# Dilation-16 attention as 64x64 products per residue class and head

## The chip, the cores and the metric

The kernel runs on one core of a Trainium2 chip. The metric is the device time of one execution in microseconds; the median of the runs shown is compared. The core has TensorE (matrix products, in the profile PE, with its weight loads as PEld), VectorE (DVE), ScalarE (ACT), GpSimd (POOL) and SyncE (SP, which issues nearly all DMAs). They run at the same time and wait for one another on semaphores.

## What is computed

Two layers of a decoder trunk on 1024 positions of 1024 features: a dilated attention mixer, an MLP, a gated linear recurrence (HGRN2), an MLP, with a layer norm after each. The change is in the attention mixer alone. It has 16 heads of 64 features and three groups with (window, dilation) = (128, 1), (512, 4), (2048, 16); the group outputs are mixed by their softmax denominators.

```
def dilated_window_attention(q, k, v, window, dilation):
    blk = window // dilation
    ...
    qb, kb, vb = to_blocks(q), to_blocks(k), to_blocks(v)   # one sequence per residue class mod dilation
    kk, vv = with_prev(kb), with_prev(vb)
    s = einsum('znqhe,znkhe->znhqk', qb, kk) * (E ** -0.5)
    s = where(valid, s, -inf)              # 0 <= distance <= blk, key exists
    m = max(s); p = exp(s - m); l = sum(p)
    o = einsum('znhqk,znkhe->znqhe', p / l, vv)
    lse = m + log(l)
```

With dilation 16 the 1024 positions fall into 16 residue classes of 64 positions. The window covers a whole class, so each class is one causal 64x64 attention and no block has a predecessor.

## The kernel before

The attention mixer is 24 units: eight pairs of heads times three dilations, in the order 16, 4, 1 within a pair (`GORD`). Two consecutive units make a group. While TensorE computes the projections of one group (21 products of twelve 128x512 passes each, lines 750 to 752), the attention work of the group before is put between these products: `unit_work` gives a list of steps, and `OFFS` says behind which product each one goes, two products (24 passes) apart. TensorE and DVE execute in the order in which the code writes them (`in_order`); ACT and SP take their instructions as the scheduler laid them.

A unit holds queries and keys of two heads with features on partitions: head 0 on partitions 0 to 63, head 1 on 64 to 127. For dilations 4 and 16 the positions are sorted by residue class, so a block of 128 columns is two classes of dilation 16. `pieces` does one unit:

- `qk` (scores, PSUM bank tag "s", two banks, one per head): for each of eight blocks b and each head a product with 64 rows of contraction and a 128x128 result. For dilation 16 half of that result is between two different classes and is masked away with the third part of `mask`. DVE (line 572) adds the mask, scales, and takes the row extreme into the statistics `sS`; ACT (line 575) takes the exponential and its row sum.
- `ptr` transposes the probabilities in four 128x128 transposes a call through a bank tagged "pt" (two banks) and copies them to an SBUF tile `pts` (line 587).
- `pv` multiplies them with the values: per block and head one product with 128 rows of contraction, 64 result partitions and 128 columns (line 598), into the one bank "o"; behind every fourth block ACT copies the bank to `og` (line 609).
- `vtrans` transposes the values (lines 545 and 546).

For dilation 16 the six steps of a unit are: 0 scores of blocks 0 to 3 and `vtrans`; 1 scores of blocks 4 to 7 and the eight transposes of the first half; 2 nothing; 3 value products of the first half and transposes of the second; 4 nothing; 5 value products of the second half. Step 5 falls on the same place as step 0 of the next unit.

`combine_tr` then transposes the statistics (line 648), writes them to DRAM (`mdram`) and reads them back in natural order into `ml`, with four DMAs on SP for dilation 16 (line 658); `combine` and `combine_mul` mix the three groups of a pair later.

Two lines outside the attention are used below: in the recurrence (`omat`) the code writes per 128 positions two products at line 1718, one to the left and one to the right 64 columns of the array, then the same two at line 1723 with the running state; in the first 128 positions only the right one of these.

In the profile an f32 product shows as two passes, an f32 transpose as one. PE shapes read as rows\*columns of the array, then the moving operand.

Of the kernel before, what the change touches and what calls it, by code (L numbers as in the profile page):

```python
# [9 lines left out]
F32 = mybir.dt.float32  # L10
F32R = mybir.dt.float32r
U8 = mybir.dt.uint8
AF = mybir.ActivationFunctionType
ALU = mybir.AluOpType
AX = mybir.AxisListType

P = 128
# [3 lines left out]
HD = 64  # L21
# [48 lines left out]
def trunk_kernel(  # L70
# [24 lines left out]
    nc = tc.nc  # L95
    cp = ctx.enter_context(tc.tile_pool(name="cp", bufs=1))
    up = ctx.enter_context(tc.tile_pool(name="up", bufs=NSLOT))
    wp = ctx.enter_context(tc.tile_pool(name="wp", bufs=3))
# [7 lines left out]
    def bank(tag, name):  # L106
        return ps.tile([P, 512], F32, name=name, tag=tag, bufs={"mm": 3, "s": 2, "pt": 2, "o": 1}[tag])

    def small(shape, name, bufs=4, dt=F32):
        return sp.tile(shape, dt, name=name, tag=name, bufs=bufs)  # L110

    act = nc.scalar.activation
# [31 lines left out]
    ident = cp.tile([P, P], F32, name="ident")  # L144
# [212 lines left out]
    def attention(pre, hc):  # L357
# [136 lines left out]
                v = nc.vector  # L494
                v.tensor_sub(H[n][:, R], lows.pop(n), H[n][:, L].bitcast(F32))  # L495

        mask = cp.tile([P, 384], F32, name="mask")
        sel = cp.tile([P, NG * P], F32R, name="bsel")
        frow = U("frow", F32R)
        mdram = dp.tile([NPAIR, NG, 2, 2, S], F32, name="mdram")  # L500
# [32 lines left out]
        def pieces(pr, g, qT, kT, vT, og, sS, tail):  # L533
            st = {}

            def has_prev(b):
                return (g == 0 and b > 0) or (g == 1 and b % 2 == 1)
# [11 lines left out]
            def qk(*tiles):  # L549
                sb = [bank("s", "s") for _ in range(2)]  # L550
                at, c0 = {}, 0
                for b in sum(tiles, ()):
                    prev = has_prev(b)
                    n = 256 if prev else 128
                    k0 = (b - 1 if prev else b) * P
                    at[b] = slice(c0, c0 + n)
                    c0 += n
                    for h in range(2):
                        nc.tensor.matmul(sb[h][:, at[b]], qT[h * HD:(h + 1) * HD, b * P:(b + 1) * P],  # L559
                                         kT[h * HD:(h + 1) * HD, k0:k0 + n], start=True, stop=True,  # L560
                                         skip_group_check=True)
                for tile_ in tiles:
                    whole = wp.tile([P, 512], F32, name="p", tag="p")
                    st["p", tile_] = whole
                    for i, b in enumerate(tile_):
                        prev = has_prev(b)
                        n = 256 if prev else 128
                        m = mask[:, 0:256] if prev else (mask[:, 256:384] if g == 2 else mask[:, 128:256])
                        p = [whole[:, (2 * i + h) * n:(2 * i + h + 1) * n] for h in range(2)]
                        for h in range(2):  # L570
                            nm = sS[:, 0, h, b:b + 1]
                            nc.vector.tensor_tensor_reduce(p[h], sb[h][:, at[b]], m, -0.125, 3.0e38,  # L572
                                                           op0=ALU.add, op1=ALU.min, accum_out=nm)
                        for h in range(2):
                            act(p[h], p[h], AF.Exp, bias=sS[:, 0, h, b:b + 1], scale=-1.0,  # L575
                                accum_out=sS[:, 1, h, b:b + 1])

            def ptr(tile_):
                pt = bank("pt", "ppt")
# [32 lines left out]
            def qks(*tiles):  # L612
                return [lambda: qk(*tiles)]

            def run(f, bs):
                return [lambda b=b: f(b) for b in bs]
# [10 lines left out]
                ]  # L627
            first, second = run(pv, range(4)), run(pv, range(4, 8))
            if g == 2:
                two = [(b, b + 1) for b in range(0, 8, 2)]  # L630
                return [qks(*two[0:2]) + [vtrans], qks(*two[2:4]) + run(ptr, two[0:2]), [],
                        first + run(ptr, two[2:4]), [], second]
            if g == 1:
                return [qks((0, 2), (4, 6)) + [vtrans], qks((1,), (3,)) + run(ptr, ((0, 2), (4, 6))),
                        qks((5,), (7,)) + run(ptr, ((1,), (3,))), first + run(ptr, ((5,), (7,))), [], second]
# [4 lines left out]
        def combine_tr(pr, g, slot, ml, tail):  # L640
            pt = bank("pt" if tail else "o", "mpt")
            q0 = slot * 32
            if DIL[g] == 1:
                for w in range(2):
                    nc.tensor.transpose(pt[:, w * P:w * P + P], allS[:, 16 * w:16 * w + P], ident)
                act(ml[:, :, 0, :], pt[0:16, 0:2 * P].rearrange("p (w t) -> p w t", w=2), AF.Copy)
                return
            nc.tensor.transpose(pt[:, 0:P], allS[:, 0:P], ident)
            sr = small([P, P], "sr", 2)
            act(sr[q0:q0 + 32], pt[q0:q0 + 32, 0:P], AF.Copy)  # L650
            yield
            md = mdram[pr, g]
            d = DIL[g]
            nc.scalar.dma_start(md.rearrange("w h (b q) -> (w h b) q", q=P), sr[q0:q0 + 32])
            yield
            for w in range(2):
                for h in range(2):
                    nc.sync.dma_start(
                        ml[8 * h:8 * h + 8, w, g, :].rearrange("i (r n) -> i r n", r=d),
                        md[w, h].rearrange("(r i n) -> i r n", r=d, i=8))  # L660
            yield

        def combine(pr, ml):
# [67 lines left out]
        ml, ogs = {}, {}  # L731
# [116 lines left out]
        for n in range(len(seq)):  # L848
            gi, i, j = seq[n]
# [1005 lines left out]
    pr = Out(w_attn_out, "a", 0)  # L1855
    hc = []
    oN, fill = attention(pr.pre_steps, hc)
    gw = GateW()
    f = ffn(0, x1d, ln_ffn_g[0], ln_ffn_b[0], False, (gw.ask, lambda: gw.prefetch(0)))
# [6 lines left out]
    f = ffn(1, x5d, ln_ffn_g[1], ln_ffn_b[1], True)  # L1866
# [6 lines left out]
def _constants():  # L1873
    import numpy as np

    f = np.float32
    half = HD // 2
    inv = (f(10000.0) ** (-np.arange(half, dtype=f) * f(2.0 / HD))).astype(f)
    ang = inv[:, None] * np.arange(S, dtype=f)[None, :]
    c, s = np.cos(ang).astype(f), np.sin(ang).astype(f)  # L1880
    cos_t = np.concatenate([c, c, c, c], 0)
    sin_t = np.concatenate([-s, s, -s, s], 0)
    qi = np.arange(P)[:, None]
    kj = np.arange(P)[None, :]
    neg = f(-1.0e30)
    prev = np.where(kj >= qi, f(0), neg)
    own = np.where(kj <= qi, f(0), neg)
    pk = np.where((kj <= qi) & (kj // 64 == qi // 64), f(0), neg)
    masks = np.concatenate([prev, own, pk], 1).astype(f)
    cm = ((kj >= qi) & (kj // CH == qi // CH)).astype(f)  # L1890
    cmask = np.tile(cm, (1, 4))
    sm = np.ones((P, S), f)
    sm[:, ::CH] = 0.0
    rows = np.arange(P)[:, None]
    bsel = np.concatenate([((rows // 4 == g) & (rows % 2 == np.arange(P)[None, :] // HD)).astype(f)
                           for g in range(NG)], 1)
    return {"cos_t": cos_t, "sin_t": sin_t, "masks": masks, "cmask": cmask, "smask": sm, "bsel": bsel}
# [49 lines left out]
```

## Time and profile before

| | |
|---|---|
| median of 3 runs | 2762.18 us (2761.52 to 2764.75) |
| profiled execution, first to last instruction (its own time as far as the profile shows it) | 2759.7 us |
| TensorE busy | 2734.4 us, 99% |
| DVE, ACT busy | 2076.6 us (75%), 1419.4 us (51%) |
| chain that ended last | PE 92%, DVE 5% |
| attention stage with its projections | from the start to about 1000 us |
| score passes (line 559), all units | 768 passes, first 84.4, last 985.6 us |
| value passes (line 598), all units | 1120 passes, first 105.0, last 993.9 us |
| transposes of probabilities (line 584) | 560 |

A row of a timeline gives the start, the time from the start of the first to the end of the last instruction of the row, engine, line, operation and count. TensorE passes overlap, so the distance between starts is what a pass costs, and it is shorter than its own duration.

### The profile page before, as it was taken

Reading aid. Unit: us, or ns where it says so; the run is one execution under the profiler, and the core shown is the slowest. Engines: PE = TensorE matmul, PEld = TensorE weight load, DVE = VectorE, ACT = ScalarE, POOL = GpSimd, SP = SyncE. Lnnn points to the kernel's source line nnn. Section 1 sums busy time; section 2 is a strip of 40 time slices with the busy share of each in tenths; the row PEclk is TensorE's granted clock in tenths of the full one; section 3 lists DMA queues with packets and bytes.
Section 4 is the critical chain, followed back from the end, with each engine's and each line's share of the span. In section 5 each row is a group of like instructions: output and inputs, shape, how many; then the busy total and the mean of one; then the engine's idle time right before and its main releaser. Section 6 shows DMA issues by size and latency. Waiting matters only on the chain.

```text
span 2759.7 us, 40110 instructions
## 1 busy us (share of the span) xinstructions
PE 2734.4 (99%) x14312; PEld 2237.2 (81%) x14312; DVE 2076.6 (75%) x3876; ACT 1419.4 (51%) x3059; POOL 69.0 (2%) x46
## 2 busy tenths in 40 slices
PE   9999999999999999999999999999999999999998
PEld 7888888888888777888888888888888888888887
DVE  8868877777888768876696777565678887678687
ACT  5555555555555456445454435455552545455443
POOL 0000000000000001000000000010100100000000
PEclk9999999999999999999999999999999999999999
DMA  8767666766767324454584852001142464485654
GB/s 303 257 209 214 197 205 191 234 185 212 225 208 226 120 94 160 168 211 152 186 290 134 275 171 92 31 32 62 65 130 104 149 220 170 143 292 191 217 176 129
DMA packets 204041, 485.02 MB, mean 176 GB/s; under 512 B 28992, under 2 KB 42816, under 8 KB 203840
## 3 DMA queue, kind: packets, MB, share of 16 engines
q1 hardware_dynamic: 203072, 482.19, 52.6%
q8 instruction: 113, 1.85, 0.3%
q14 instruction: 88, 0.72, 0.1%
q10 hardware_dynamic: 768, 0.26, 0.0%
HBM read 362.69 MB, written 94.11 MB: 166 GB/s over the span
## 4 chain that ended last, share of the span: by engine, by line
PE 92%; DVE 5%; ACT 1%; issue 1%; DMA 1%; SPq 0%; POOL 0%; DVEq 0%; ACTq 0%; POOLq 0%
PE pmm L752 8%; PE pmm L750 8%; PE pmm L751 8%; PE pup L1272 7%; PE pup L1270 7%; PE pup L1271 7%; PE pdy L1421 4%; PE pdy L1425 4%; PE pdy L1424 4%; PE pdx L1424 3%; PE pdx L1425 3%; PE pdx L1421 3%; PE pmm L192 3%; PE pmm L194 3%; PE pmm L193 3%; PE s L559 3%
## 5 line engine op out<-in xcount | busy, mean ns | idle before, releaser
L750 PE MATMUL pmm<-xh,H 128*128 128x512 f32 x1008 | 402.1, 399 | 2.0 <-ACT H L487 1.9
L752 PE MATMUL pmm<-xh,H 128*128 128x512 f32 x1008 | 394.0, 391 | 2.3 <-DVE H L495 2.2
L751 PE MATMUL pmm<-xl,H 128*128 128x512 f32 x1008 | 393.0, 390 | 0.7 <-DVE xl L158 0.7
L752 PEld LDWEIGHTS pmm<-xh,H 128*128 128x128 f32 x1008 | 189.2, 188 | 44.9 <-DVE H L495 4.3
L750 PEld LDWEIGHTS pmm<-xh,H 128*128 128x128 f32 x1008 | 189.5, 188 | 40.4 <-ACT H L487 3.0
L751 PEld LDWEIGHTS pmm<-xl,H 128*128 128x128 f32 x1008 | 189.7, 188 | 37.7 <-DVE xl L158 1.1
L575 ACT ACTIVATE p<-p,stats 128x128 f32<-128x128 f32 (+1 forms) x384 | 167.9, 440 | 81.6 <-DVE stats L572 81.4
L1421 PE MATMUL pdy<-dT,dS 128*128 128x512 f32 x512 | 199.2, 389 | 0.0
L1424 PE MATMUL pdy<-dT,dS 128*128 128x512 f32 x512 | 199.2, 389 | 0.0
L1425 PE MATMUL pdy<-dT,dS 128*128 128x512 f32 x512 | 199.2, 389 | 0.0
L572 DVE CUSTOM_DVE_ANT_0 p<-s,mask 128x128 f32<-128x128 f32 (+1 forms) x384 | 111.1, 348 | 98.9 <-PE s L559 91.0
L157 ACT ACTIVATE dS<-dr 128x512 fp32r<-128x512 f32 x192 | 119.4, 622 | 69.9 <-PE pdy L1425 36.2
L192 PE MATMUL pmm<-f0nh,wh 128*128 128x512 f32 x384 | 153.2, 399 | 0.0
L194 PE MATMUL pmm<-f0nh,wl 128*128 128x512 f32 x384 | 149.8, 390 | 0.0
L193 PE MATMUL pmm<-f0nl,wh 128*128 128x512 f32 x384 | 149.7, 390 | 0.0
L158 DVE TENSOR_TENSOR dS<-dr,dS 128x512 fp32r<-128x512 f32 x192 | 131.5, 685 | 7.6 <-ACT dS L157 7.6
L157 ACT ACTIVATE dT<-hold 128x512 fp32r<-128x512 f32 x128 | 80.1, 626 | 78.5 <-DVE hold L1400 33.4
L1231 ACT ACTIVATE H<-wc 128x512 fp32r<-128x512 f32 x128 | 77.2, 626 | 77.6 <-DVE wc L1224 46.4
L1425 PEld LDWEIGHTS pdy<-dT,dS 128*128 128x128 f32 x512 | 96.1, 188 | 20.1
L1424 PEld LDWEIGHTS pdy<-dT,dS 128*128 128x128 f32 x512 | 96.1, 188 | 19.9
L1421 PEld LDWEIGHTS pdy<-dT,dS 128*128 128x128 f32 x512 | 96.1, 188 | 19.8
L587 ACT ACTIVATE pts<-ppt 128x512 f32<-128x512 f32 (+1 forms) x146 | 77.7, 575 | 44.4 <-PE ppt L584 44.1
(412 smaller groups left out, 6836.0 us busy)
## 6 DMA issues: line engine op xcount, KB each, us to landing
xh<-xtd SPq DMA_DIRECT2D x110, 512.0 KB
xl<-xtd SPq DMA_DIRECT2D x110, 512.0 KB
dr<-hd SPq DMA_DIRECT2D x192, 256.0 KB
dr<-in_w_down_dram SPq DMA_DIRECT2D x128, 256.0 KB
rot<-e SPq DMA_DIRECT2D x192, 128.0 KB
wa<-in_w_up_dram SPq DMA_DIRECT2D x48, 512.0 KB
wb<-in_w_attn_dram SPq DMA_DIRECT2D x36, 512.0 KB
wa<-in_w_attn_dram SPq DMA_DIRECT2D x33, 512.0 KB
```

Of the source, the lines that this page charges most:

```text
L157: act(hi, raw, AF.Copy)
L192: nc.tensor.matmul(o, wh[:, k], xs.h(k), start=k == 0, stop=False)
L193: nc.tensor.matmul(o, wh[:, k], xs.l(k), start=False, stop=False)
L194: nc.tensor.matmul(o, wl[:, k], xs.h(k), start=False, stop=k == NK - 1)
L750: nc.tensor.matmul(o, wh, hi[k // 2][:, c], start=begin and k == 0, stop=False, skip_group_check=True)
L751: nc.tensor.matmul(o, wh, lo[k // 2][:, c], start=False, stop=False, skip_group_check=True)
L752: nc.tensor.matmul(o, wl, hi[k // 2][:, c], start=False, stop=end and k == 3, skip_group_check=True)
L1270: nc.tensor.matmul(o, wh, xf.h(b, k), start=begin and k == 0, stop=False, skip_group_check=True)
L1271: nc.tensor.matmul(o, wh, xf.l(b, k), start=False, stop=False, skip_group_check=True)
L1421: nc.tensor.matmul(o[q], h, T_[:, L], start=begin, stop=False, skip_group_check=True)
L1424: nc.tensor.matmul(o[q], h, T_[:, R], start=False, stop=False, skip_group_check=True)
L1425: nc.tensor.matmul(o[q], l, T_[:, L], start=False, stop=end, skip_group_check=True)
```

## The change

For dilation 16 alone, `qk`, `ptr` and `pv` are replaced by `qk16`, `ptr16` and `pv16`. A block's two classes (cl = 0, 1) are computed apart, so that no masked quarter is computed. Scores are products of 64 rows, 64 result partitions and 64 columns: the head sets the row half of the array, and head xor class the column half, so the bank of a class holds both heads, one on each partition half. DVE and ACT thus treat both heads of a class in one instruction of 64 columns. The two classes of a block stand side by side in a 128x128 piece of the probabilities, and one transpose serves both heads and both classes. In the value products the class sets the row half and the head the column half; one bank per class, the second taken from the tag "pt". The six steps become: 0 scores of the first half and `vtrans`; 1 scores of the second half and transposes of the first; 2 transposes of the second; 3 all value products and both copies; 4 and 5 nothing. Since the statistics now lie by class with the heads on partition halves, the read-back is eight DMAs of half the size. The mask shrinks from 384 to 320 columns.

TensorE at step 1 of the unit of pair 1. `s` are scores, `ppt` transposes, `pmm` the projection's passes; xN counts products. Before:

```order
L751 MATMUL pmm<-xl,H 128x512
L752 MATMUL pmm<-xh,H 128x512
L559 MATMUL s<-kT,qT 128x128 x8
L584 MATMUL ppt<-ident,p 128x128 x8
L750 MATMUL pmm<-xh,H 128x512
```

and after:

```order
L798 MATMUL pmm<-xl,H 128x512
L799 MATMUL pmm<-xh,H 128x512
L587 MATMUL s<-kT,qT 64x64 x16
L603 MATMUL ppt<-ident,p 128x128 x4
L797 MATMUL pmm<-xh,H 128x512
```

Twice as many score products of a quarter of the size, and four transposes, of the first half's probabilities, where there were eight.

TensorE at step 2, where the kernel before has only projection passes. After:

```order
L798 MATMUL pmm<-xl,H 128x512
L799 MATMUL pmm<-xh,H 128x512
L603 MATMUL ppt<-ident,p 128x128 x4
L797 MATMUL pmm<-xh,H 128x512
L798 MATMUL pmm<-xl,H 128x512
```

Four transposes have moved here from step 3; their scores are two projection products earlier, not four.

TensorE at step 3, `o` being the value products. Before:

```order
L751 MATMUL pmm<-xl,H 128x512
L752 MATMUL pmm<-xh,H 128x512
L598 MATMUL o<-pts,vn 64x128 x8
L584 MATMUL ppt<-ident,p 128x128 x8
L750 MATMUL pmm<-xh,H 128x512
```

and after:

```order
L798 MATMUL pmm<-xl,H 128x512
L799 MATMUL pmm<-xh,H 128x512
L615 MATMUL o<-pts,vn 64x64 x32
L797 MATMUL pmm<-xh,H 128x512
L798 MATMUL pmm<-xl,H 128x512
```

All 32 value products stand in one place, in turns over the two banks. The eight of step 5, which stood ahead of the next unit's scores, are gone from there.

The diff:

```diff
--- before.py
+++ after.py
@@ -494,7 +494,7 @@
                 v = nc.vector
                 v.tensor_sub(H[n][:, R], lows.pop(n), H[n][:, L].bitcast(F32))
 
-        mask = cp.tile([P, 384], F32, name="mask")
+        mask = cp.tile([P, 320], F32, name="mask")
         sel = cp.tile([P, NG * P], F32R, name="bsel")
         frow = U("frow", F32R)
         mdram = dp.tile([NPAIR, NG, 2, 2, S], F32, name="mdram")
@@ -565,7 +565,7 @@
                     for i, b in enumerate(tile_):
                         prev = has_prev(b)
                         n = 256 if prev else 128
-                        m = mask[:, 0:256] if prev else (mask[:, 256:384] if g == 2 else mask[:, 128:256])
+                        m = mask[:, 0:256] if prev else mask[:, 128:256]
                         p = [whole[:, (2 * i + h) * n:(2 * i + h + 1) * n] for h in range(2)]
                         for h in range(2):
                             nm = sS[:, 0, h, b:b + 1]
@@ -574,6 +574,50 @@
                         for h in range(2):
                             act(p[h], p[h], AF.Exp, bias=sS[:, 0, h, b:b + 1], scale=-1.0,
                                 accum_out=sS[:, 1, h, b:b + 1])
+
+            def qk16(j):
+                sb = [bank("s", "s") for _ in range(2)]
+                whole = wp.tile([P, 512], F32, name="p", tag="p")
+                blocks = [(b, cl, slice((b % 4 * 2 + cl) * 64, (b % 4 * 2 + cl) * 64 + 64))
+                          for b in range(4 * j, 4 * j + 4) for cl in range(2)]
+                for b, cl, c in blocks:
+                    q = slice(b * P + cl * 64, b * P + cl * 64 + 64)
+                    for h in range(2):
+                        r = slice(h * HD, (h + 1) * HD)
+                        nc.tensor.matmul(sb[cl][(h ^ cl) * HD:(h ^ cl) * HD + HD, b % 4 * 64:b % 4 * 64 + 64],
+                                         qT[r, q], kT[r, q], start=True, stop=True, skip_group_check=True)
+                for b, cl, c in blocks:
+                    nc.vector.tensor_tensor_reduce(whole[:, c], sb[cl][:, b % 4 * 64:b % 4 * 64 + 64],
+                                                   mask[:, 256:320], -0.125, 3.0e38, op0=ALU.add, op1=ALU.min,
+                                                   accum_out=sS[:, 0, cl, b:b + 1])
+                for b, cl, c in blocks:
+                    act(whole[:, c], whole[:, c], AF.Exp, bias=sS[:, 0, cl, b:b + 1], scale=-1.0,
+                        accum_out=sS[:, 1, cl, b:b + 1])
+                st["p", j] = whole
+
+            def ptr16(j):
+                pt = bank("pt", "ppt")
+                pts = wp.tile([P, 512], F32, name="pts", tag="pts", bufs=4)
+                p = st.pop(("p", j))
+                for i in range(4):
+                    nc.tensor.transpose(pt[:, i * P:(i + 1) * P], p[:, i * P:(i + 1) * P], ident)
+                act(pts, pt, AF.Copy)
+                st["pt", j] = pts
+
+            def pv16():
+                o = [bank(tag, "o") for tag in ("o", "pt")]
+                for b in range(8):
+                    pts = st["pt", b // 4]
+                    for cl in range(2):
+                        r = slice(cl * 64, cl * 64 + 64)
+                        for h in range(2):
+                            m = b % 4 * P + (h ^ cl) * 64
+                            nc.tensor.matmul(o[cl][h * HD:(h + 1) * HD, b * 64:b * 64 + 64],
+                                             st["vn"][r, b * P + h * HD:b * P + (h + 1) * HD], pts[r, m:m + 64],
+                                             start=True, stop=True, skip_group_check=True)
+                for cl in range(2):
+                    act(og.rearrange("p (n b x) -> p x b n", b=8, x=2)[:, cl],
+                        o[cl].rearrange("p (b n) -> p b n", b=8), AF.Copy)
 
             def ptr(tile_):
                 pt = bank("pt", "ppt")
@@ -627,9 +671,8 @@
                 ]
             first, second = run(pv, range(4)), run(pv, range(4, 8))
             if g == 2:
-                two = [(b, b + 1) for b in range(0, 8, 2)]
-                return [qks(*two[0:2]) + [vtrans], qks(*two[2:4]) + run(ptr, two[0:2]), [],
-                        first + run(ptr, two[2:4]), [], second]
+                return [run(qk16, (0,)) + [vtrans], run(qk16, (1,)) + run(ptr16, (0,)), run(ptr16, (1,)),
+                        [pv16], [], []]
             if g == 1:
                 return [qks((0, 2), (4, 6)) + [vtrans], qks((1,), (3,)) + run(ptr, ((0, 2), (4, 6))),
                         qks((5,), (7,)) + run(ptr, ((1,), (3,))), first + run(ptr, ((5,), (7,))), [], second]
@@ -655,9 +698,13 @@
             yield
             for w in range(2):
                 for h in range(2):
-                    nc.sync.dma_start(
-                        ml[8 * h:8 * h + 8, w, g, :].rearrange("i (r n) -> i r n", r=d),
-                        md[w, h].rearrange("(r i n) -> i r n", r=d, i=8))
+                    to = ml[8 * h:8 * h + 8, w, g, :].rearrange("i (r n) -> i r n", r=d)
+                    if g == 2:
+                        for cl in range(2):
+                            nc.sync.dma_start(to.rearrange("i (b x) n -> i x b n", x=2)[:, cl],
+                                              md[w, cl].rearrange("(b x i n) -> x i b n", x=2, i=8, n=8)[h ^ cl])
+                        continue
+                    nc.sync.dma_start(to, md[w, h].rearrange("(r i n) -> i r n", r=d, i=8))
             yield
 
         def combine(pr, ml):
@@ -1885,7 +1932,7 @@
     neg = f(-1.0e30)
     prev = np.where(kj >= qi, f(0), neg)
     own = np.where(kj <= qi, f(0), neg)
-    pk = np.where((kj <= qi) & (kj // 64 == qi // 64), f(0), neg)
+    pk = np.where(kj[:, :64] <= qi % 64, f(0), neg)
     masks = np.concatenate([prev, own, pk], 1).astype(f)
     cm = ((kj >= qi) & (kj // CH == qi // CH)).astype(f)
     cmask = np.tile(cm, (1, 4))
```

## The prediction

> **What bounds the kernel now.** I read the page's sums first, then the stretches of the attention stage, then TensorE's own order in time around one dilation-16 unit, and last the groups by shape.
>
> ```profile
> PE 2734.4 (99%) x14312; PEld 2237.2 (81%) x14312; DVE 2076.6 (75%) x3876; ACT 1419.4 (51%) x3059; POOL 69.0 (2%) x46
> ...
> PE 92%; DVE 5%; ACT 1%; issue 1%; DMA 1%; SPq 0%; POOL 0%; DVEq 0%; ACTq 0%; POOLq 0%
> ```
>
> The whole program is TensorE, and so is the stage that the change touches. In the row of stretches the columns are the stretch, then busy time of PE, PEld, DVE, ACT and POOL, the granted clock, the DMA share and GB/s:
>
> ```profile
> 80.00:940.00 860.00, 859.45 (x5225) 697.55 (x5223) 675.22 (x1490) 494.98 (x1328) 0.96 (x1) 1.00 0.66 210
> ```
>
> From 80 to 940 us, where all eight dilation-16 units lie, PE is busy 859.45 of 860 us at clock 1.00. So each microsecond taken off TensorE here comes off the end, as long as no other engine turns late, and whatever is taken off DVE (675 us) or ACT (495 us) is worth nothing by itself.
>
> Next the unit (pair 1, dilation 16) and, ahead of it, the end of the unit before, in TensorE's order of time:
>
> ```profile
> 190.77 0.39 PE L752 MATMUL pmm<-xh,H 128*128 128x512 f32 x1
> 191.00 1.03 PE L584 MATMUL ppt<-ident,p 128*128 128x128 f32 x8
> 191.87 0.38 PE L645 MATMUL mpt<-ident,stats 128*128 128x128 f32 x2
> 192.01 0.48 PE L750 MATMUL pmm<-xh,H 128*128 128x512 f32 x1
> ...
> 197.65 1.97 PE L598 MATMUL o<-pts,vn 128*64 128x128 f32 x32
> 199.55 1.16 PE L559 MATMUL s<-kT,qT 64*128 64x128 f32 x16
> ...
> 206.82 0.39 PE L752 MATMUL pmm<-xh,H 128*128 128x512 f32 x1
> 207.14 1.16 PE L559 MATMUL s<-kT,qT 64*128 64x128 f32 x16
> 208.23 1.09 PE L584 MATMUL ppt<-ident,p 128*128 128x128 f32 x8
> 209.08 0.47 PE L750 MATMUL pmm<-xh,H 128*128 128x512 f32 x1
> 209.39 0.39 PE L751 MATMUL pmm<-xl,H 128*128 128x512 f32 x1
> ...
> 219.85 0.39 PE L752 MATMUL pmm<-xh,H 128*128 128x512 f32 x1
> 220.16 1.09 PE L598 MATMUL o<-pts,vn 128*64 128x128 f32 x16
> 221.19 1.09 PE L584 MATMUL ppt<-ident,p 128*128 128x128 f32 x8
> 222.04 0.47 PE L750 MATMUL pmm<-xh,H 128*128 128x512 f32 x1
> ...
> 235.68 0.39 PE L752 MATMUL pmm<-xh,H 128*128 128x512 f32 x1
> 236.00 1.09 PE L598 MATMUL o<-pts,vn 128*64 128x128 f32 x16
> 237.02 1.16 PE L559 MATMUL s<-kT,qT 64*128 64x128 f32 x16
> 238.12 1.09 PE L545 MATMUL vpt<-ident,vT 128*128 128x128 f32 x8
> 238.96 0.48 PE L750 MATMUL pmm<-xh,H 128*128 128x512 f32 x1
> ```
>
> Durations overlap, so I price by starts. Attention work stands in small packets between the projection's 128x512 passes, and no packet holds a wait. An f32 product is two passes (eight score products give x16). Four prices follow:
> - o: 32 passes take 199.55 - 197.65 = 1.90, 16 take 221.19 - 220.16 = 1.03: 0.0544 us a pass and 0.16 fixed for the change of shape.
> - s: 16 passes take 208.23 - 207.14 = 1.09; at 0.056 a pass that is 0.19 fixed.
> - transposes: eight take 191.87 - 191.00 = 0.87, 0.109 each.
> - A packet lengthens the first projection pass behind it by 0.08 (209.08 to 209.39, where 0.23 is usual).
>
> **What a pass pays for.** The trace has no 64-column f32 pass, so its price must be bounded. Two facts decide. The first is width:
>
> ```profile
> 126.76 1.14 PE L559 MATMUL s<-kT,qT 64*128 64x256 f32 x8
> 127.82 1.09 PE L584 MATMUL ppt<-ident,p 128*128 128x128 f32 x8
> ...
> L598 PEld LDWEIGHTS o<-pts,vn 128*64 128x64 f32 x1120 | 60.2, 136 | 18.2 <-issue 17.1 <-ACT og L609 1.1
> L559 PEld LDWEIGHTS s<-kT,qT 64*128 64x128 f32 x768 | 56.0, 186 | 22.7 <-issue 15.7 <-DVE vT L775 1.1 <-DVE H L495 1.1
> ```
>
> Eight score passes of 256 columns take 1.06 us, sixteen of 128 take 1.09: time goes by columns, not by passes. A weight load goes by columns too (64 columns 136 ns, 128 columns 186: 50 ns for 64 more). So neither a 64-column pass nor its load needs over about 55 ns in its own part of the array.
>
> The second is how many parts run at once. Today two do (s in two row halves, o in two column halves): 0.0544 a pass is half of the 0.109 that 128 f32 columns take alone, as the transposes show. That the parts keep queues of their own is seen in the recurrence, where the code writes per block two products at L1718 (left and right column half) and then L1723, in the first block for the right half only:
>
> ```profile
> 1921.19 0.54 PE L1718 MATMUL ho<-vn,aT 128*64 128x128 f32 x5
> 1921.47 0.27 PE L1723 MATMUL ho<-stA,qe 128*64 128x128 f32 x1
> 1921.57 0.27 PE L1718 MATMUL ho<-vn,aT 128*64 128x128 f32 x1
> 1921.58 0.38 PE L1723 MATMUL ho<-stA,qe 128*64 128x128 f32 x2
> ```
>
> Written order is four L1718 passes, then L1723; the chip starts a fifth L1718, the next block's left half, before the first L1723. A half that is free goes ahead, and two passes start 0.01 us apart. The new code walks all four quarters in turn (row half by head or class, column half by head), so I take four at once, each with half of the 0.112 that a score pass takes in its own half, and 0.001 for the turn: 0.057 / 4 = 0.0143 us a pass. The ends of the range: 0.0272 if two run at once as now, 0.0544 if a 64-column pass costs what a 128-column one does. I lean to the first, since width and independence each have a row here and a fixed cost per pass has none.
>
> **The change, per dilation-16 unit** (eight of them, one per pair; steps 0 to 5 are the places of its lists):
> - Step 0, scores: 16 passes become 32 of 64 columns. 0.19 + 32 x 0.0143 = 0.65 against 1.09: -0.44.
> - Step 1, scores the same -0.44; transposes 8 to 4: -0.44.
> - Step 2, new packet of four transposes alone: ten cost 192.01 - 190.77 less one usual 0.23 = 1.01, so four cost 1.01 - 6 x 0.109 = 0.36, with 0.08 behind: +0.44.
> - Step 3, 2.19 from 219.85 to 222.04 becomes 0.31 (to the first o) + 0.16 + 64 x 0.0143 = 1.39, all the value products and no transposes: -0.80.
> - Step 5, the second half of the value products is gone from a packet shared with the next unit: 236.00 to 237.02, -1.02.
> - Sum -2.70, times eight -21.6 us.
>
> Off the path: per unit 16 mask passes on DVE and 16 exponentials on ACT go from 128 to 64 columns, pts copies from 4 to 2, the two og copies stay but come together; that relieves two engines that have room. The second o bank now comes from the two "pt" banks and is held for two og copies; the next user of that bank is a projection product (2.7 us) or more away, so nothing. On SP the read-back of the statistics is 8 DMAs instead of 4, each half as large:
>
> ```profile
> L658 SPq DMA_DIRECT2D ml<-mdram x64: 276/322/1124, 120.7 to 988.3; - x64
> ```
>
> Four more at 0.32 is 1.3 us of SP per pair, ahead of the next xl or rot load. PE waits for no load in this stage (row 80:940), so I take 0; without that cover it is at most 8 x 1.3 = 10 us. The smaller mask load is nothing.
>
> The one new dependency is tighter: the second half's transposes stood four projection products behind their scores (step 3), now two (step 2). A projection pass is 0.227 (10.46 us from 209.39 to 219.85 hold 46 of them). From score start to that packet are 0.65 + 0.44 + 0.08 + 24 x 0.227 = 6.6 us, and 0.3 more to the last transpose. The last exponential today:
>
> ```profile
> 92.00 1.16 PE L559 MATMUL s<-kT,qT 64*128 64x128 f32 x16
> ...
> 100.70 0.39 ACT L575 ACTIVATE p<-p,stats 128x128 f32<-128x128 f32 x1
> 100.99 0.19 ACT L575 ACTIVATION_READ_ACCUMULATOR p<-p,stats 128x1 f32 x1
> ...
> 326.44 1.16 PE L559 MATMUL s<-kT,qT 64*128 64x128 f32 x16
> ...
> 332.49 0.39 ACT L575 ACTIVATE p<-p,stats 128x128 f32<-128x128 f32 x1
> 332.78 0.19 ACT L575 ACTIVATION_READ_ACCUMULATOR p<-p,stats 128x1 f32 x1
> ```
>
> It ends 6.5 us after the scores start in the unit at 326, 9.2 in the first one. Eight exponentials of 64 columns and shorter scores take some 0.4 each off that: about 5.7 and 8.3. Only the first unit waits, 8.3 - 6.9 = about 1.3 us. Total -20.3 us. The profiled span is 2759.7, 2.5 us below the median of the runs; against the median 2762.2 that is 2742 us.
>
> **Rivals.**
> - B, a bank at a time. In a score packet the quarters (rows 0-63, columns 0-63) and (rows 64-127, columns 64-127) write one PSUM bank; today two row halves always write two. If two row halves may not share a bank, scores run two at a time: 32 x 0.0272 + 0.19 = 1.06, and steps 0 and 1 lose 0.41 each, 6.6 in all: 2749 us. For it: no row here shows two row halves in one bank. Against: the two write different partitions. The Trainium skill, "TensorEngine Tiling (Array Packing)", section Gotcha 1: PSUM Pressure, says that different row tiles cannot access the same PSUM bank simultaneously; by that rule the time would be B's.
> - C, two at a time, or a fixed cost per pass near 0.027: scores 1.06, step 3 becomes 0.31 + 0.16 + 64 x 0.0272 = 2.21. The sum is -0.03 -0.03 -0.44 +0.44 +0.02 -1.02 = -1.06, -8.5 in all, less the wait: 2755 us. Instructions per unit rise from 48 products to 72, and no row shows how fast TensorE takes them. The Trainium skill, "TensorE: Matmul & The Clock Gate", section Back-to-back issue gap, gives about 25 ns from start to start for up to 64 columns; as an estimate from that page the time would be about 2753 us, and the 0.01 us between starts in the rows above speaks against it within a burst.
> - D, slower: a pass costs its 0.0544 whatever its width. Scores 0.19 + 32 x 0.0544 = 1.93 (+0.84 twice), step 3 0.47 + 3.48 = 3.95 (+1.76), the rest as above: +2.42 a unit, 2783 us. The sum changes sign at about 0.035 a pass: 128 passes weigh 128 x 0.035 = 4.5, what the rest saves. Against it are the widths above.
> - E, slower by waits: the transposes of step 2 would have to wait 2.7 us in every unit. The exponentials would have to end 9.6 us after the scores start; only the first unit comes near.
>
> **How the numbers follow.** A (four at once) 0.56, B 0.12, C with rates between A and C 0.17, D 0.07, E 0.03, no measurable change by a mixture 0.05. Prediction 2742 us. The low end, 2738, is A with no wait and 0.3 less per unit for the changes of shape; the high end, 2757, is C with one or two microseconds of waits. About 0.2% (5.5 us) is what a measurement of this kernel tells from no change, so faster (below 2756.7) takes A, B and most of C: 0.84; same 0.06; slower 0.10.
>
> **What would show it.** Right: s packets of dilation 16 about 0.65 us to the next start, 64 o passes in about 1.1 us, a lone packet of four transposes, PE still over 99% busy from 80 to 920 us, and attention ending some 20 us earlier. Wrong: o passes 0.03 us apart or more (C, D); s slower per pass than o (B); PE idle ahead of the transposes with exponentials as releaser (E); or PE waiting for xl loads behind the statistics' read-back.

## The result and the profile after

| | before | after |
|---|---|---|
| median, same chip | 2762.39 us (4 runs) | 2743.73 us (4 runs, 2742.70 to 2744.95) |
| ratio | | 0.9934, 95% interval 0.9922 to 0.9946 |
| profiled execution | 2759.7 us | 2740.9 us |
| the changed kernel run again, in another series | 2761.75 us | 2745.21 us, ratio 0.9938 (0.9924 to 0.9951), profiled 2743.4 us |

The changed kernel is 18.7 us faster (16.5 in the second series); 2742 was predicted. Below, "the changed kernel" is 2744.5 us, the mean of the two medians. The other runs come from three series, in which the kernel before takes 2761.31, 2761.75 and 2762.43 us; a microsecond more or less between series means nothing.

The page of the changed kernel, its sums and its chain:

```profile
PE 2714.7 (99%) x14760; PEld 2218.5 (81%) x14760; DVE 2069.9 (76%) x3876; ACT 1402.9 (51%) x3043; POOL 68.9 (3%) x46
...
PE 90%; DVE 7%; ACT 2%; issue 1%; DMA 1%; SPq 0%; POOL 0%; DVEq 0%; ACTq 0%; POOLq 0%
```

TensorE is busy 19.7 us less and is still busy 99% of the time, although it now takes 448 instructions more. The stretch from the first scores to the last projection pass, which holds all dilation-16 work but the last unit's value products, in the same columns as before (stretch, then busy PE, PEld, DVE, ACT, POOL, clock, DMA share, GB/s):

```profile
85.00:910.20 825.20, 824.11 (x5557) 666.83 (x5557) 648.89 (x1467) 470.99 (x1297) 0.96 (x1) 1.00 0.68 213
```

PE stands still for 1.1 us in 825. The saving is therefore in what PE executes, and the place to read it is PE's own order in time. The changed kernel's timeline on PE has the same unit (pair 1) from 196 us on; the first unit's lone transposes and the last projection pass of the stage stand around it:

```profile
98.72 0.38 PE L603 MATMUL ppt<-ident,p 128*128 128x128 f32 x2
...
100.02 0.33 PE L603 MATMUL ppt<-ident,p 128*128 128x128 f32 x1 [0.33 <-ACT p L594]
100.10 0.48 PE L797 MATMUL pmm<-xh,H 128*128 128x512 f32 x1
...
198.47 0.69 PE L587 MATMUL s<-kT,qT 64*64 64x64 f32 x32
...
199.95 0.48 PE L797 MATMUL pmm<-xh,H 128*128 128x512 f32 x1
...
205.60 0.69 PE L587 MATMUL s<-kT,qT 64*64 64x64 f32 x32
206.22 0.66 PE L603 MATMUL ppt<-ident,p 128*128 128x128 f32 x4
206.63 0.48 PE L797 MATMUL pmm<-xh,H 128*128 128x512 f32 x1
...
211.97 0.39 PE L799 MATMUL pmm<-xh,H 128*128 128x512 f32 x1
212.20 0.60 PE L603 MATMUL ppt<-ident,p 128*128 128x128 f32 x4
212.55 0.48 PE L797 MATMUL pmm<-xh,H 128*128 128x512 f32 x1
212.87 0.40 PE L798 MATMUL pmm<-xl,H 128*128 128x512 f32 x1
...
218.22 1.16 PE L615 MATMUL o<-pts,vn 64*64 64x64 f32 x64
219.31 0.50 PE L797 MATMUL pmm<-xh,H 128*128 128x512 f32 x1
...
233.29 1.16 PE L559 MATMUL s<-kT,qT 64*128 64x128 f32 x16
...
235.23 0.47 PE L797 MATMUL pmm<-xh,H 128*128 128x512 f32 x1
...
240.88 1.13 PE L559 MATMUL s<-kT,qT 64*128 64x256 f32 x8
242.20 1.14 PE L628 MATMUL ppt<-ident,p 128*128 128x128 f32 x8 [0.19 <-ACT vn L546]
243.09 0.48 PE L797 MATMUL pmm<-xh,H 128*128 128x512 f32 x1
...
910.45 0.39 PE L799 MATMUL pmm<-xh,H 128*128 128x512 f32 x1
```

Three rows of before that were not needed until now: the end of the packet with step 0's scores, the packet that answers to 240.88, and the last projection pass.

```profile
201.49 0.48 PE L750 MATMUL pmm<-xh,H 128*128 128x512 f32 x1
...
244.61 1.14 PE L559 MATMUL s<-kT,qT 64*128 64x256 f32 x8
...
246.53 0.47 PE L750 MATMUL pmm<-xh,H 128*128 128x512 f32 x1
...
927.52 0.39 PE L752 MATMUL pmm<-xh,H 128*128 128x512 f32 x1
```

Each packet, from its first attention pass of the unit to the next projection pass:

| | before | after | difference | predicted |
|---|---|---|---|---|
| step 0, from the scores | 201.49 - 199.55 = 1.94 | 199.95 - 198.47 = 1.48 | -0.46 | -0.44 |
| step 1 | 209.08 - 207.14 = 1.94 | 206.63 - 205.60 = 1.03 | -0.91 | -0.88 |
| step 2, lone transposes | | 212.87 - 211.97, less two usual passes of 0.227 | +0.45 | +0.44 |
| step 3 | 222.04 - 220.16 = 1.88 | 219.31 - 218.22 = 1.09 | -0.79 | -0.80 |
| step 5, shared with the next unit | 238.96 - 236.00 = 2.96 | 235.23 - 233.29 = 1.94 | -1.02 | -1.02 |
| sum | | | -2.73 | -2.70 |

The other units' packets take the same within 0.02 us, apart from the waits and the last unit's end that are told further below.

The price per pass is what the prediction took: 64 value passes take 1.09, less 0.16 fixed, 0.0145 us each; 32 score passes take 206.22 - 205.60 = 0.62, less 0.19, 0.0134 each. The fixed part need not be taken from the prediction: 32 value passes alone take 0.63 in the run with the value products alone (below), so the other 32 cost 1.09 - 0.63 = 0.46, or 0.0144 each. All four quarters of the array run at once: single starts in this trace come in fours, 0.007 us apart, and the next four start 0.058 us after the first.

### The profile page after: what moved, and what is told of

Its sections match the earlier page's. It is cut to its first block, busy times and chain, and to the rows that moved or that the text cites. A ratio compares the mean times of both kernels' runs of the same rounds, so it can differ in the third digit from the quotient of the medians.

```text
span 2740.9 us, 41042 instructions
## 1 busy us (share of the span) xinstructions
PE 2714.7 (99%) x14760; PEld 2218.5 (81%) x14760; DVE 2069.9 (76%) x3876; ACT 1402.9 (51%) x3043; POOL 68.9 (3%) x46
## 4 chain that ended last, share of the span: by engine, by line
PE 90%; DVE 7%; ACT 2%; issue 1%; DMA 1%; SPq 0%; POOL 0%; DVEq 0%; ACTq 0%; POOLq 0%
PE pmm L797 7%; PE pmm L799 7%; PE pmm L798 7%; PE pup L1319 7%; PE pup L1317 7%; PE pup L1318 7%; PE pdy L1471 4%; PE pdy L1468 4%; PE pdy L1472 4%; PE pdx L1471 3%; PE pdx L1472 3%; PE pdx L1468 3%; PE pmm L192 3%; PE pmm L194 3%; PE pmm L193 3%; PE ppt L628 2%
## 5 line engine op out<-in xcount | busy, mean ns | idle before, releaser
L575 ACT ACTIVATE p<-p,stats 128x256 f32<-128x256 f32 (+1 forms) x256 | 118.3, 465 | 72.8 <-DVE stats L572 72.1
L572 DVE CUSTOM_DVE_ANT_0 p<-s,mask 128x256 f32<-128x256 f32 (+1 forms) x256 | 82.7, 380 | 58.4 <-PE s L559 49.0
L1278 ACT ACTIVATE H<-wc 128x512 fp32r<-128x512 f32 x128 | 77.2, 625 | 77.2 <-DVE wc L1271 47.9
L487 ACT ACTIVATE H<-wc 128x512 fp32r<-128x512 f32 x108 | 66.6, 630 | 70.4 <-DVE wc L479 53.8
```

## The experiments

**Two quarters instead of four.** The only change is which column half a score product writes, so that it is always the head's:

```diff
-   nc.tensor.matmul(sb[cl][(h ^ cl) * HD:(h ^ cl) * HD + HD, b % 4 * 64:b % 4 * 64 + 64],
+   nc.tensor.matmul(sb[cl][h * HD:h * HD + HD, b % 4 * 64:b % 4 * 64 + 64],
```

(and the places where the probabilities and the statistics are read). Work, banks and instruction counts stay; row half and column half now go together, so the scores never use two of the four quarters.

> The changed kernel with the head alone setting the column half in the scores, so that scores use only two quarters of the array (rows and columns 0-63, rows and columns 64-127); the value products still use all four. Theory (four quarters run side by side and a pass costs its columns): 32 score passes go from about 0.65 us to 0.19 + 32 x 0.027 = 1.06 us in each of 16 packets, +6.6 us on 2743.7: 2750.3. Rival (the gain of the scores does not come from the number of quarters, for instance because passes were held by their number or by waits): 2743.7, packets as in the changed kernel.

Measured: 2751.23 us, ratio to before 0.9965 (0.9951 to 0.9979), 6.7 us above the changed kernel. The timeline at step 1:

```profile
207.37 1.15 PE L587 MATMUL s<-kT,qT 64*64 64x64 f32 x32
208.45 0.66 PE L603 MATMUL ppt<-ident,p 128*128 128x128 f32 x4
```

The scores take 1.08 where the changed kernel's take 0.62. Less 0.19 that is 0.028 a pass, twice the price. Sixteen packets at 0.46 are 7.4 us, and 6.7 were measured. So the price is set by how many quarters work, not by a fixed cost per pass. Rival B falls on the changed kernel itself: its four quarters write only two banks, two row halves each, so 0.0134 us a pass is reached only if two row halves write one bank at the same time.

**Score products class by class.** The same 16 products in another written order, all of class 0 and then all of class 1. Each class uses two quarters:

```diff
-                for b, cl, c in blocks:
+                for b, cl, c in sorted(blocks, key=lambda t: t[1]):
                     q = slice(b * P + cl * 64, b * P + cl * 64 + 64)
```

> The changed kernel with the scores of a packet written class by class: 16 passes that use one pair of quarters, then 16 that use the other pair. Theory, if a quarter's queue is served whatever stands ahead of it for other quarters: TensorE still runs all four and nothing moves, 2743.7 and 0.65 us a score packet. Rival, if passes start in written order up to a short look-ahead: two at a time, 1.06 us a packet and 2750.3.

The same place (step 1 of pair 1's unit) in this kernel's timeline of PE:

```profile
206.26 0.97 PE L587 MATMUL s<-kT,qT 64*64 64x64 f32 x32
207.17 0.66 PE L603 MATMUL ppt<-ident,p 128*128 128x128 f32 x4
```

Measured: 2748.59 us, ratio 0.9955 (0.9941 to 0.9969); the scores take 0.91, 0.29 more than in the changed order. Sixteen times 0.29 are 4.6 us; 4.1 were measured. Neither expectation holds: TensorE does go ahead to a free quarter, but only some passes far. The trace shows it on the pass that raises the semaphore for class 0's finished scores: it is written 16th of the 32 and starts 21st. (In the run with two quarters the pass with this semaphore is written 28th and starts 28th.) A model that starts, of the oldest six passes not yet started, the first whose quarter is free, at 0.057 us per pass in a quarter, gives 0.285. The six is fitted to this run, so it needed tests of its own, the next two runs.

**Products twice.** Every score and value product of dilation 16 is issued twice, the second over the first (here the scores; the value products alike).

```diff
                     for h in range(2):
                         r = slice(h * HD, (h + 1) * HD)
-                        nc.tensor.matmul(sb[cl][(h ^ cl) * HD:(h ^ cl) * HD + HD, b % 4 * 64:b % 4 * 64 + 64],
+                        for _ in range(2):
+                          nc.tensor.matmul(sb[cl][(h ^ cl) * HD:(h ^ cl) * HD + HD, b % 4 * 64:b % 4 * 64 + 64],
```

> The changed kernel with every score product and every value product of dilation 16 issued twice in a row into the same place. 32 more passes in each of 16 score packets and 64 more in each of 8 value packets, 1024 in all. Theory (0.0143 us a pass): +14.6 us, 2758.3; score packets 1.1, value packets 2.0 us. Rival (passes start no faster than one in 0.025 us when more than a queue's worth stands in a row): +25.6, 2769.3. Rival (two at a time): +28 us.

The timeline of PE at steps 1 and 3 of this kernel:

```profile
208.77 1.30 PE L588 MATMUL s<-kT,qT 64*64 64x64 f32 x64
210.01 0.66 PE L604 MATMUL ppt<-ident,p 128*128 128x128 f32 x4
...
221.99 2.24 PE L617 MATMUL o<-pts,vn 64*64 64x64 f32 x128
224.16 0.50 PE L799 MATMUL pmm<-xh,H 128*128 128x512 f32 x1
```

Measured: 2761.23 us, 16.7 above the changed kernel. The 32 more score passes cost 1.24 - 0.62 = 0.62, 0.019 each; the 64 more value passes 2.17 - 1.09 = 1.08, 0.017 each. That is far from the rivals and a little above 0.0143: with each product twice, four passes in a row want the same quarter, and the others lie further ahead. The model gives 0.62 and 1.13 for the two, with 0.007 us between two starts as in the traces (0.57 and 1.03 without). It fits the length of the packets, not each start: in this trace the first four passes start within 0.040 us. If a quarter starts one pass in 0.058 us, these four are of four quarters, and the last of them is written 13th, beyond a look-ahead of six.

**Classes by pairs of blocks.** Two blocks of one class, the same two of the other, and so on:

```diff
-                for b, cl, c in blocks:
+                for b, cl, c in sorted(blocks, key=lambda x: (x[0] // 2, x[1])):
```

> The changed kernel, with the score products written two blocks of one class, then the same two blocks of the other class. A model in which TensorE starts, of the oldest six passes not yet started, the first whose quarter is free (0.057 us per pass in a quarter) gives 0.06 us more per score packet than the changed order (3.69 and 1.36 become 3.75 and 1.41), where class by class for four blocks it gave 0.285. With a look-ahead of eight or more passes it would be 0.00, of five 0.11, and without one, two quarters at a time, 0.41. The total should be within 1.5 us of the changed kernel's.

Step 1 again, in this kernel's timeline of PE:

```profile
205.72 0.74 PE L587 MATMUL s<-kT,qT 64*64 64x64 f32 x32
206.40 0.66 PE L603 MATMUL ppt<-ident,p 128*128 128x128 f32 x4
```

One run, 2744.32 us. The scores take 0.68, 0.06 more than in the changed order: what a look-ahead of six or seven passes gives in the model, and not eight (0) or five (0.11). A single run says little of the total, but in its trace the last projection pass comes at 911.33, 0.88 later than in the changed kernel, and sixteen times 0.06 are 0.96. Another model does as well: each quarter holds three passes, the running one included, and is filled in written order. It gives 0.285 class by class, 0.63 and 1.08 for products twice, and 0.06 here, and it does not explain the four first starts either. So that passes go ahead is shown; the rule by which they do stays open.

**Transposes twice.** In the changed kernel each transpose of the dilation-16 probabilities is issued twice:

```diff
-                for i in range(4):
+                for i in (0, 1, 2, 3, 0, 1, 2, 3):
```

> The changed kernel, with every transpose of the dilation-16 probabilities issued twice (the second to the same place with the same data), 64 more of them in all, 0.109 us each by the rows of before: 64 x 0.109 = 7.0 us. If transposes are on the path at that price, the lone packet grows from 0.59 to 1.02 us, the packet of step 1 from 1.36 to 1.79, and the time from about 2744.5 to about 2751.5 us; that would put 7 of the 18 us saved down to the halved transposes. Rival: the weight loads and the idle parts around a packet hide some of it, and the time rises by 3 us or less.

The lone transposes of step 2 and the projection pass behind them, in this kernel's timeline of PE:

```profile
213.08 1.04 PE L603 MATMUL ppt<-ident,p 128*128 128x128 f32 x8
213.87 0.48 PE L797 MATMUL pmm<-xh,H 128*128 128x512 f32 x1
```

Measured: 2751.29 us, ratio 0.9961 (0.9947 to 0.9975), 6.8 above the changed kernel; the lone packet grows from 0.35 to 0.79. Transposes are wholly on the path at 0.109 each, and the eight that a unit no longer has are worth the 7 us expected. With the scores' 16 x 0.46 = 7.4 that leaves of 8 x 2.73 = 21.8 some 7.4 for the value products: three nearly equal parts.

**Value products alone.** The kernel before, with only its value products cut into quarters, half a unit at step 3 and half at step 5, each into the bank "o" and one "pt" bank:

```diff
+            def pvq(half):
+                o = [bank(tag, "o") for tag in ("o", "pt")]
...
-                        first + run(ptr, two[2:4]), [], second]
+                        run(pvq, (0,)) + run(ptr, two[2:4]), [], run(pvq, (1,))]
```

> The kernel before with one part of the change: scores, masks and 16 transposes stay 128 wide, only the value products are 64x64 on four quarters, eight blocks in two halves at the old steps 3 and 5, two banks and two half-size copies each. Theory: each half takes 0.16 + 32 x 0.0143 = 0.62 us where 1.03 stood, -0.41 in 16 packets: -6.6 us, 2755.8 against 2762.4 before. Rival (what the value products gave came from doing all of them in one packet): no change, 2762.4. Four copies of 256 columns instead of two of 512 load ACT a little more; that should not show.

Step 3 in this kernel's timeline of PE, with the wait in brackets:

```profile
220.75 0.69 PE L620 MATMUL o<-pts,vn 64*64 64x64 f32 x32
221.38 0.66 PE L584 MATMUL ppt<-ident,p 128*128 128x128 f32 x4
222.57 0.66 PE L584 MATMUL ppt<-ident,p 128*128 128x128 f32 x4 [0.54 <-ACT og L624]
222.99 0.48 PE L765 MATMUL pmm<-xh,H 128*128 128x512 f32 x1
```

Measured: 2763.23 us, ratio 1.0006 (0.9997 to 1.0014): no gain, and the expectation failed. Step 5 does what was expected (its packet takes 2.56 instead of 2.97), and step 3 loses as much again. There the passes are as cheap as expected (221.38 - 220.75 = 0.63 for 32), but the transposes behind them, in the same packet, need both "pt" banks, and one is held by "o" until ACT has copied it. The packet takes 222.99 - 220.75 = 2.24 instead of 1.88; in other units it takes 2.38, and the wait there is for the copy of the other "pt" bank (to `pts`).

**Value products alone, other bank.** The same, with step 3's second bank from the tag "s":

```diff
-                o = [bank(tag, "o") for tag in ("o", "pt")]
+                o = [bank(tag, "o") for tag in (("o", "pt") if half else ("o", "s"))]
```

> The kernel before with the value products alone cut into quarters, as in the run with the value products alone, but the second bank of step 3 comes from the tag s, which nothing else in that packet uses; step 5 keeps the tag pt. If that run's gain was eaten up only by the pt bank, which the transposes of the same packet needed, the packet of step 3 should now fall from 2.19 to about 1.8 us (0.41 less), as the packet of step 5 did, with no wait on the og copies left in it: 16 x 0.41 = 6.6 us less than before, about 2755 us. Rival: value products in quarters beside transposes cost more for another reason (the change of shape between them): the packet of step 3 stays at 2.2 us or above and the time at 2761 or more.

Step 3 in this kernel's timeline of PE, and the end of the packet of step 5:

```profile
220.00 0.69 PE L620 MATMUL o<-pts,vn 64*64 64x64 f32 x32
220.63 1.09 PE L584 MATMUL ppt<-ident,p 128*128 128x128 f32 x8
221.48 0.47 PE L765 MATMUL pmm<-xh,H 128*128 128x512 f32 x1
...
237.16 0.66 PE L545 MATMUL vpt<-ident,vT 128*128 128x128 f32 x4
238.22 0.66 PE L545 MATMUL vpt<-ident,vT 128*128 128x128 f32 x4 [0.41 <-ACT og L624]
```

Measured: 2759.12 us, ratio 0.9990 (0.9981 to 0.9999), 3.3 faster than before; 6.6 were expected. Step 3 does what was expected: the packet takes 221.48 - 220.00 = 1.48, 0.40 less, without a wait. Step 5 still has "pt", and in three of the seven units that meet the next unit there, the next unit's transposes of values now wait for that bank, as the last row shows; these three packets take 0.61 more than the others of step 5. The last unit's two packets lie in the output projection (see below). That leaves 14 x 0.40 - 3 x 0.61 = 3.8 of the 6.6. Bank and packet together decide what a cheaper pass is worth.

**Later steps.** The changed kernel with the second half's transposes one step later and the value products behind them, to remove the first unit's wait:

```diff
-                return [run(qk16, (0,)) + [vtrans], run(qk16, (1,)) + run(ptr16, (0,)), run(ptr16, (1,)),
-                        [pv16], [], []]
+                return [run(qk16, (0,)) + [vtrans], run(qk16, (1,)) + run(ptr16, (0,)), [],
+                        run(ptr16, (1,)), [pv16], []]
```

> The changed kernel with the second half's transposes at step 3 instead of 2 and the value products at step 4 instead of 3. Theory: the first unit's wait ahead of these transposes (about 1 us in the trace of the changed kernel) goes, nothing else: 2742.7, within what a measurement can tell. Rival (the tight step costs more than the trace shows, or later value products make something late): more than 3 us either way.

The timeline of PE, and from its list of waits (total us, times, longest) the largest:

```profile
225.41 1.16 PE L615 MATMUL o<-pts,vn 64*64 64x64 f32 x64
227.69 0.33 PE L691 MATMUL mpt<-ident,stats 128*128 128x128 f32 x1 [1.11 <-ACT og L619]
```

```profile
PE mpt L691 <- ACT og L619: 10.5, 7, 2.0
```

Measured: 2760.39 us, ratio 0.9996 (0.9987 to 1.0005), 15 us slower than the changed kernel in the same series: a clear miss. The first unit's wait was gone, but the statistics' transpose now stands right behind the value products, and it needs the bank "o", which the copies to `og` hold. Seven waits, 10.5 of the 15 us; one wait of 2.0 us for `H` at 493 us was not there before, and the rest was not followed.

**Sixteen read-back DMAs.** The eight of the changed kernel are each cut in two.

```diff
                         for cl in range(2):
-                            nc.sync.dma_start(to.rearrange("i (b x) n -> i x b n", x=2)[:, cl],
+                            for j in range(2):
+                                js = slice(4 * j, 4 * j + 4)
+                                nc.sync.dma_start(
+                                    to.rearrange("i (b x) n -> i x b n", x=2)[js, cl],
...
```

> The changed kernel with the read-back of the dilation-16 statistics in sixteen DMAs of four rows instead of eight of eight rows. Theory (SP has room, TensorE waits for no load in this stage): no change, 2743.7. Rival (each DMA's 0.3 us on SP delays the next load and TensorE): 8 more DMAs a pair cost up to 2.6 us, 20 us in all, and the change itself paid half of that.

SP's queue and DVE behind the read-back of pair 1, first in this kernel, then in the changed kernel, and last this kernel's waits of PE for `H` from 85 us to the last projection pass:

```profile
237.22 5.60 SPq L706 DMA_DIRECT2D ml<-mdram  x16
...
251.78 1.23 DVE L530 TENSOR_TENSOR rot<-rot,sinT 128x1024 f32<-128x1024 f32 x1 [4.24 <-DMA rot<-e]
```

```profile
237.79 2.81 SPq L704 DMA_DIRECT2D ml<-mdram  x8
...
249.41 1.23 DVE L530 TENSOR_TENSOR rot<-rot,sinT 128x1024 f32<-128x1024 f32 x1 [1.31 <-DMA rot<-e]
```

```profile
PE pmm L802 <- DVE H L495: 1.6, 3, 0.8
```

Measured: 2747.79 us, ratio 0.9951 (0.9938 to 0.9963), 2.6 above the changed kernel in the same series. The read-back holds SP's queue for 5.60 us instead of 2.81, and the loads of `rot` stand behind it. DVE gets `rot` 2.4 us later, and since it works in written order the `H` behind `rot` and `qT` comes later too: PE waits 0.67 us for it at 254.92. Two more such waits, at 486.23 and 718.20, make 1.6 us. Neither the changed kernel nor the kernel before has a wait for `H` in this stretch, so eight DMAs are covered and sixteen are not. The other 1.0 us was not followed.

## Why the prediction was right, point by point

- **What bounds the kernel, and four quarters at once:** right, and shown by the run with two quarters and by the two packets' own rows. Rivals B, C and D fall with it. The Trainium skill's rule for B ("TensorEngine Tiling (Array Packing)", section Gotcha 1: PSUM Pressure) is not what happens here: two row halves write different partitions of one bank at 0.0134 us a pass. Nor does the Trainium skill's floor of about 25 ns from start to start ("TensorE: Matmul & The Clock Gate", section Back-to-back issue gap), behind C, hold between products in different quarters: there starts follow at 7 ns.
- **The terms of the sum:** each within 0.03 us, -2.73 against -2.70 per unit. One reading on the way does not follow from its rows: that a 64-column weight load needs no more than about 55 ns. The row has 136 ns for such a load, and the 512 loads of line 587 last 135 ns (median). Eight of these in a quarter fit into a packet of 0.62 us only because they overlap, so the price came out right for another reason than the one given.
- **The first unit's wait:** the only one for exponentials, as predicted, but 1.0 us instead of 1.3. The lone packet there takes 100.10 - 98.72 = 1.38 against 212.55 - 212.20 = 0.35.
- **A wait that was not foreseen:** three times about 0.3 us, at step 1 of the dilation-4 unit behind a dilation-16 unit that is the second of its group. At 240.88 the packet takes 243.09 - 240.88 = 2.21, before 246.53 - 244.61 = 1.92. The transposes wait for a "pt" bank whose copy to `vn` ACT makes late (the changed kernel's timeline of ACT):

```profile
241.57 1.06 ACT L546 ACTIVATE vn<-vpt 128x512 f32<-128x512 f32 x2
```

  The packet on PE comes 3.73 us earlier than before (240.88 against 244.61), this copy only 2.07 (241.57 against 243.64). Ahead of the copy ACT works off the exponentials of step 0, which follow the mask passes on DVE, and DVE works without a pause here: the first exponential also comes only 2.07 us earlier (238.47 against 240.54). So the change took more time off PE than off DVE, and the next unit met DVE's lag. That is read from the trace and was not tried alone.
- **The last unit:** its steps 3 and 5 were counted at 1.8 us like the others'. The prediction read 80 to 940 us as one stretch without waits that holds all eight units, but the projections end at 927.52. These two steps lie behind it, in the output projection, where PE also waits for other things, and they bought nothing there. The stretch behind the last projection pass, before and then after, in the columns of the stretches above:

```profile
927.00:1009.60 82.60, 79.61 (x490) 59.30 (x489) 61.02 (x145) 43.39 (x118) 0.00 (x0) 1.00 0.33 106
```

```profile
910.20:992.70 82.50, 79.06 (x512) 58.29 (x511) 61.04 (x145) 42.05 (x116) 0.00 (x0) 1.00 0.34 106
```

  It takes 82.50 us instead of 82.60. The account up to the last projection pass: steps 0 to 2 of eight units, 8 x (-0.46 - 0.91 + 0.45) = -7.4; steps 3 and 5 of seven, 7 x -1.81 = -12.7; waits +1.0 and +0.9: -18.2. Measured: 910.45 - 927.52 = -17.1. The first scores already start 0.6 later (85.0 against 84.4), so -17.7 belongs to the stage, and 0.5 is unexplained. The program's end is 18.8 earlier, in the second profile of the changed kernel 16.3, though the two agree within 0.1 us at that pass: what is left behind the attention stage, in parts that the change does not touch, varies by that much, and no cause was sought. So of the first series' 18.7 us about one is luck: the attention stage gave 17 to 18 of the 20.3 forecast, and the second series measured 16.5.
- **The second o bank "so nothing":** right for the changed kernel, since its packet with value products has no transposes. The two runs with the value products alone show that this was the condition, and the prediction did not state it.
- **Read-back at 0:** right for eight DMAs. The bound of 10 us for four more a pair was far off, since the next eight a pair cost 2.6 us in all. What PE came to wait for stood behind the load of `rot`, not behind that of `xl`, which the prediction had named as the sign.

No run beat the changed kernel. Taking the first unit's wait away by later steps cost far more than it saved.

## What to carry to other kernels

Cut small products so that all four quarters of TensorE's array have work, and write them in turn, since TensorE goes to a free quarter only a few passes ahead. Read the price of a packet from start to start in the timeline, and before a product takes a PSUM bank of another tag, see which instruction of the same packet or right behind it needs that tag. A shorter packet brings PE sooner to the next wait: look up how late the engine stands that releases the bank there.

## What the hardware showed that was not expected

- f32 passes of 64 rows and 64 columns in four quarters cost 0.0134 to 0.0145 us each, and 0.028 when two quarters do the work; they start in fours 0.007 us apart, 0.015 us in the mean over a packet.
- Passes start out of their written order when their quarter is free: class by class, the pass written 16th starts 21st, and the packet takes 0.91 us, where two quarters at a time take 1.08. The Trainium skill, "TensorE: Matmul & The Clock Gate", section Step-by-step: what each phase is for, says that products stay in program order and only weight loads go ahead; between quarters these rows speak against it.
- How far they go ahead stays open. A look-ahead of six, fitted to one run (0.29 us class by class), meets the packets of two others: 0.62 and 1.08 for products twice (model 0.62 and 1.13), 0.06 for pairs of blocks (model 0.06). Queues of three passes per quarter meet them as well, and neither gives the first starts of the products-twice packet.
